# Attention output split from its accumulation bank into projection operands; gate tiles by block; chain sums by transfer

## The chip, the cores and the metric

The kernel runs on one core of a Trainium2 chip. The metric is device time in microseconds (us) of one execution. The engines are TensorE (PE, with its weight loads PEld), VectorE (DVE), ScalarE (ACT), GpSimd (POOL, which here mostly issues transfers) and SyncE (SP, which issues the loads and stores). Every engine works through its own queue of instructions in order; the queues meet at semaphores.

## The reference

One step of a layer of a streaming encoder in float32, over T = 16 + 1024 + 32 = 1072 tokens (16 meta tokens, 1024 frames of a new stream, 32 frames of a running one), model width 1024:

```python
h = rmsnorm(x, g)
a_in, q, k, v = split(h @ w_in, [1024, 1536, 1664])          # ONE input projection, 1792 columns
glu  = a_in[..., :512] * sigmoid(a_in[..., 512:])
a    = silu(layernorm(depthwise_causal_conv(glu, width=31)))  # group A, 512 channels
# group B: 8 query heads, 2 key/value heads of 64; chunks of 64 tokens see the 16 meta
# tokens, the two chunks before and their own; a bias by distance; one sink per head
s = q @ k.T * 64**-0.5 + bias
m = maximum(max(s), sink);  p = exp(s - m)
o = (p / (sum(p) + exp(sink - m))) @ v
x = x + concat([a, o]) @ w_out                                # 1024 x 1024
u = rmsnorm(x) @ w_up                                         # 2 x 2816 columns
x = x + (silu(depthwise_causal_conv(u[:2816], width=3)) * u[2816:]) @ w_down
y = rmsnorm(x)
```

The new keys, values and convolution states are outputs too.

## The kernel before

**Layout.** All activations are feature-major: 128 partitions of features, so that 1024 features are eight k-tiles, and tokens along the free axis. Tokens go in three blocks, 336, 384 and 352 wide in the input projection (`TB`) and 324, 384 and 352 (the chunks' own borders: `OB`) or with their halos in the stages behind it.

**Precision.** Each float32 operand of a large product is two parts: `hi`, a cast to a narrower form of float32 that PE takes in one pass, and `lo`, the rest. A k-step of such a product is three matmuls, hi by hi, lo by hi and hi by lo (`mm3`, L255 to L257). `hi` is always a cast on ACT. `lo` is made in one of two ways: by a subtraction on DVE (`split`, L249 and L250; for weights L242), or by a negation on ACT (L244) and a transfer from POOL's queue that adds the raw operand to it.

**Input projection.** Its 14 column tiles of 128 are the keys, the values, four of queries, and for each of the four channel tiles of group A a value and a gate tile. Twelve are done ahead of the attention loop. The last two, gate and value of channel tile 3, are a generator, `glu_stream`, which the attention loop draws on for k-steps to fill PE. It does all three blocks of the one tile, then all three of the other. When a block's sums are ready, ACT and DVE turn them into gated values (`flush`), and the convolution taps of this channel and block can start.

**Convolution.** 31 taps on DVE for each channel tile and token range, each one multiply-add over a row of up to 1090 values (L400 for the first, L403 for the others). They are put into DVE's queue at a lower priority than all else, so the scheduler places them where it expects DVE to be free. A table `TA` says how many microseconds' worth of taps each iteration of the loop may bring. For one channel tile, the taps 1 to 20 of its second and third block are made in another way, the "chain": ACT multiplies, and transfers add the products up in the halves of a buffer. At the end of iteration `CHE` = 5 two DVE additions (L434) add these sums to the accumulator.

**The attention loop.** Eighteen jobs (the meta tokens, eleven chunks, the running stream, five chunks), and two more iterations to drain, as a pipeline of three stages. Iteration i does, in this written order:

1. for job i-1: the reciprocals of the softmax sums on DVE (L769), and the normalisation of four probability tiles, the last `SCA[i]` of them on ACT (L774), the others on DVE (L772);
2. for job i: the scores on PE (L802), bias and row minimum on DVE (L757), the exponentials on ACT (L764);
3. for job i-2: the value products on PE (L837, L841), into one half of the accumulation bank called `o`; the two halves take turns from job to job;
4. for job i-1: the transposes of the probabilities on PE (L821, L823) and their copy to the operand of the value product on ACT (L828);
5. for job i-2: `keep`, which copies the value products from the bank into the float32 buffer `CA` on ACT (L845);
6. `FILL[i]` k-steps of `glu_stream`, the evacuation of sums that are ready, and `taps(TA[i])`.

In this region PE and ACT go in the written order, and DVE in the order that the scheduler chose. When `glu_stream` has ended, the iterations go on with the generator `later` (it closes the pool "h" that holds the input projection's operands `hi` and `lo`, opens the pools of the next stage in its place, and prepares weights) and with the first groups of the output projection's attention half, block 0.

**From the loop to the output projection.** `ca_split` (L935, L936, L940) turns `CA` block by block into the operands `CAH` and `CAL`: for block 0's first half and block 1's second half by ACT (cast and negation) and an adding transfer, otherwise by ACT's cast and DVE's subtraction (L250). `later` calls it for blocks 0 and 1 inside the loop, and for block 2 it is called behind the loop. The attention half of the output projection follows (PE, mainly), with the convolution's layer norm beside it, then its convolution half, then the feed-forward part.

The lines that matter most here:

```python
def keep(self, t=None, n=64):
    nc.scalar.copy(CA[:, :, self.tok:self.tok + n],
                   self.o[:, :4 * n].rearrange("p (a b) -> p a b", a=4))
def chain_end():
    for a, half in chain:
        nc.vector.tensor_tensor(out=a, in0=a, in1=half, op=ALU.add)
```

Of the kernel before, what the change touches and what calls it, by code (L numbers as in the profile page):

```python
# [54 lines left out]
TA = [2.01, 2.74, 5.63, 6.64, 4.22, 3.28, 2.42, 2.68, 2.08, 1.57, 2.08, 2.08, 3.18, 1.41, 2.1, 0.85, 4.71, 3.21, 5.98, 2.57]  # L55
# [17 lines left out]
SCA = [1, 2, 2, 2, 1, 1, 2, 2, 2, 2, 2, 1, 2, 2, 0, 1, 1, 2, 2, 2]  # L73
# [6 lines left out]
CHE = 5  # L80
# [4 lines left out]
CSD = ['12', '00']  # L85
AH = (1, 2, 1, 3, 5, 4, 5)
AG = (('00', '02'), ('h',), ('l',), ('10',), ('12',))
# [82 lines left out]
def body(nc, tc, cp, wp, xp, dp, io):  # L170
# [36 lines left out]
    cH, ph = pool("h", "right")  # L207
    HI, LO = [None] * 3, [None] * 3
    for z, name, b in ((HI, "hi", 0), (HI, "hi", 2), (LO, "lo", 2), (HI, "hi", 1), (LO, "lo", 1), (LO, "lo", 0)):
        z[b] = new(ph, f"{name}{b}", KD, TB[b][1], dt=F32R)  # L210
# [221 lines left out]
    def chain_end():  # L432
        for a, half in chain:
            nc.vector.tensor_tensor(out=a, in0=a, in1=half, op=ALU.add)  # L434
        chain.clear()
# [352 lines left out]
    class Chunk:  # L788
# [55 lines left out]
        def keep(self, t=None, n=64):  # L844
            nc.scalar.copy(CA[:, :, self.tok:self.tok + n],  # L845
                           self.o[:, :4 * n].rearrange("p (a b) -> p a b", a=4))
# [65 lines left out]
    def glu_stream():  # L912
        w = nxt
        for i, c in enumerate(order[NPRE:]):
            for b in range(3):
                for k, ps in enumerate(in_mm(b, w, lead(c, b))):
                    if k == 2 and b == 0:
                        wn = take()
                    if k == 2 and b == 1:
                        fetch()  # L920
# [3 lines left out]
            w = wn  # L924
        woas.append(w)
# [3 lines left out]
    CAH, CAL, woas = [], [], []  # L929

    def ca_split(b, k0, k1, dma=False):
        t0, n = OB[b]
        for k in range(k0, k1):
            if dma:
                nc.scalar.copy(CAH[b][:, k, :], CA[:, k, t0:t0 + n])  # L935
                nc.scalar.activation(CAL[b][:, k, :], CA[:, k, t0:t0 + n], AF.Copy, scale=-1.0)  # L936
            else:
                split(CAH[b][:, k, :], CAL[b][:, k, :], CA[:, k, t0:t0 + n])
        if dma:
            nc.gpsimd.dma_start(CAL[b][:, k0:k1, :], CA[:, k0:k1, t0:t0 + n], accum_op=ALU.add)  # L940

    def after_glu():
# [8 lines left out]
        for step in AG:  # L951
            for op in step:
# [9 lines left out]
                else:  # L962
                    while op[0] == "1" and kept[0] < 11:
                        yield
# [933 lines left out]
```

## Time and profile before

| | |
|---|---|
| runs | 1049.37, 1050.64, 1051.31 us (median 1050.64) |
| profiled execution | 1049.64 us, its span 1047.9 us |
| PE, PEld busy | 1030.4 us (98%), 1004.3 us |
| DVE, ACT, POOL busy | 864.3 us (82%), 507.0 us (48%), 163.8 us (16%) |
| transfers | 124.41 MB, 119 GB/s in the mean |
| attention loop | from 163.5 us (first scores) to 248.3 us (last value products) |

The span is the time from the first to the last instruction that the profile holds; what lies around it (1.74 us here) belongs to the execution too. Line numbers are those of the kernel before. In a row of a window or a timeline the first figure is the start in us and the second the duration. In a row of a group of instructions, the figures behind the bar are the busy time in us, the mean duration of one in ns, and the idle time of the engine just ahead of them, with what ended most of it.

### The profile page before, as it was taken

How to read it: one execution, taken by the hardware profiler on the slowest of the kernel's cores; microseconds unless marked ns; L12 is line 12 of the kernel's file. 1: busy time of each engine (PE TensorE's matmuls, PEld its weight loads, DVE VectorE, ACT ScalarE, POOL GpSimd, SP SyncE). 2: the span in 40 equal slices, each digit the busy share in tenths (PEclk: the TensorE clock that was granted, in tenths of full speed). 3: DMA queues.
4: the chain of work that ended last, by engine and by line, in shares of the span. 5: the costliest groups of instructions: out<-in, count | busy, mean ns of one | idle time of the engine just before them, and what ended most of it. 6: DMA issues, size and time to landing. Idle time of an engine off the chain costs nothing.

```text
span 1047.9 us, 19995 instructions
## 1 busy us (share of the span) xinstructions
PE 1030.4 (98%) x7747; PEld 1004.3 (96%) x7747; DVE 864.3 (82%) x1649; ACT 507.0 (48%) x1074; POOL 163.8 (16%) x205
## 2 busy tenths in 40 slices
PE   9999999989999999999999999999999999999997
PEld 8999998758999999999999999999999999999997
DVE  7999988899978978878888888888777976986636
ACT  8653336896675644433333343343336722532334
POOL 1133220002335210001000110100010041000043
PEclk9999999999999999999999999999999999999999
DMA  7388673124953213242233234232326795732204
GB/s 268 90 172 163 147 152 79 41 55 72 171 152 109 68 63 102 76 140 93 72 124 113 64 101 116 89 103 85 120 72 210 247 190 127 247 125 68 95 2 166
DMA packets 69047, 124.41 MB, mean 119 GB/s; under 512 B 10448, under 2 KB 42568, under 8 KB 68952
## 3 DMA queue, kind: packets, MB, share of 16 engines
q1 hardware_dynamic: 56392, 97.77, 28.9%
q0 software_dynamic: 12128, 24.95, 14.0%
q8 instruction: 61, 1.00, 0.4%
q10 hardware_dynamic: 432, 0.41, 0.1%
q14 instruction: 34, 0.28, 0.1%
HBM read 79.42 MB, written 27.51 MB: 102 GB/s over the span
## 4 chain that ended last, share of the span: by engine, by line
PE 86%; ACT 6%; DVE 6%; DMA 2%; issue 1%; SPq 0%; DVEq 0%; ACTq 0%
PE mm L1282 51%; PE mm L255 10%; PE mm L256 10%; PE mm L257 10%; ACT pb L764 1%; DVE acc L403 1%; ACT glu L828 1%; DVE bl L1219 1%; DVE x L1424 1%; PE R L292 1%; ACT hi L341 1%; PE R L271 1%; DMA xs<-xT 0%; DMA gx<-yq 0%; ACT glu L764 0%
## 5 line engine op out<-in xcount | busy, mean ns | idle before, releaser
L1282 PE MATMUL mm<-bh,sl 128*128 128x264 f32 (+1 forms) x912 | 214.0, 284 | 0.0
L1282 PEld LDWEIGHTS mm<-bh,sl 128*128 128x128 f32 x912 | 157.2, 188 | 0.0
L403 DVE SCALAR_TENSOR_TENSOR acc<-glu,prm,acc 128x324 f32<-128x324 f32 (+4 forms) x190 | 155.3, 846 | 1.1
L1282 PE MATMUL mm<-bl,sl 128*128 128x264 f32 (+1 forms) x424 | 120.9, 285 | 0.0
L1282 PE MATMUL mm<-th,rawr 128*128 128x264 f32 x640 | 120.0, 284 | 0.0
L1282 PE MATMUL mm<-bh,wlo 128*128 128x264 f32 (+1 forms) x440 | 117.6, 284 | 0.0
L1424 DVE TENSOR_TENSOR x<-x,mm 128x264 f32<-128x264 f32 (+7 forms) x238 | 76.8, 351 | 44.4 <-PE mm L1282 44.3
L1282 PE MATMUL mm<-bh,whi 128*128 128x264 f32 (+1 forms) x440 | 112.6, 284 | 0.7 <-DVE x L1424 0.7
L255 PE MATMUL mm<-hi,whi 128*128 128x352 f32 (+3 forms) x312 | 103.9, 333 | 0.4 <-ACT hi L341 0.4
L256 PE MATMUL mm<-lo,whi 128*128 128x352 f32 (+3 forms) x312 | 101.2, 324 | 0.2 <-DVE lo L342 0.2
L257 PE MATMUL mm<-hi,wlo 128*128 128x352 f32 (+3 forms) x312 | 101.2, 324 | 0.0
L1282 PEld LDWEIGHTS mm<-th,rawr 128*128 128x128 f32 x640 | 100.4, 188 | 0.0
L1282 PE MATMUL mm<-th,sl 128*128 128x264 f32 x352 | 92.7, 284 | 0.0
L1282 PE MATMUL mm<-tl,rawr 128*128 128x264 f32 x320 | 90.8, 284 | 0.0
L1282 PEld LDWEIGHTS mm<-bh,wlo 128*128 128x128 f32 x440 | 80.6, 188 | 0.0
L1282 PEld LDWEIGHTS mm<-bl,sl 128*128 128x128 f32 x424 | 79.9, 188 | 0.0
L1282 PEld LDWEIGHTS mm<-bh,whi 128*128 128x128 f32 x440 | 79.0, 188 | 0.9 <-issue 0.9
L1282 PE MATMUL mm<-bl,whi 128*128 128x264 f32 (+1 forms) x272 | 77.5, 285 | 0.0
L1218 ACT CAST sl<-x 128x512 fp32r<-128x512 f32 (+1 forms) x41 | 29.7, 727 | 73.2 <-DMA x<-wup 37.6
L1282 PEld LDWEIGHTS mm<-th,sl 128*128 128x128 f32 x352 | 63.8, 188 | 0.0
L1282 PEld LDWEIGHTS mm<-tl,rawr 128*128 128x128 f32 x320 | 60.3, 188 | 0.0
L255 PEld LDWEIGHTS mm<-hi,whi 128*128 128x128 f32 x312 | 58.7, 188 | 1.6 <-issue 0.6
(400 smaller groups left out, 2925.7 us busy)
## 6 DMA issues: line engine op xcount, KB each, us to landing
x<-wup SPq DMA_DIRECT2D x20, 512.0 KB, 4.1
x<-wup SPq DMA_DIRECT2D x40, 256.0 KB, 2.8
yq<-x SPq DMA_DIRECT2D x32, 264.0 KB, 2.8
wlo<-raw POOLq DMA_DIRECT2D x16, 512.0 KB, 4.6
ca<-ca POOLq DMA_DIRECT2D x18, 383.0 KB, 5.1
raw<-win SPq DMA_DIRECT2D x12, 512.0 KB, 4.4
raw<-wdn SPq DMA_DIRECT2D x12, 512.0 KB, 3.5
rb<-yq SPq DMA_DIRECT2D x10, 528.0 KB, 4.4
```

Of the source, the lines that this page charges most:

```text
L255: nc.tensor.matmul(ps, whi(k), xhi(k), start=first and i == 0, stop=False)
L256: nc.tensor.matmul(ps, whi(k), xlo(k), start=False, stop=False)
L257: nc.tensor.matmul(ps, wlo(k), xhi(k), start=False, stop=last and i == n - 1)
L271: nc.tensor.matmul(ss[:, i:i + 1], z[:, at:at + P], ones[:, 0:1], start=j == 0, stop=j == len(parts) - 1)
L292: nc.tensor.matmul(R[:, at:at + P], left[i], diag[i], start=True, stop=True)
L341: hid[b, k] = nc.scalar.activation(HI[b][:, k, :], X[b][:, k, :], AF.Copy, scale=pcol("g1", k)).ins
L403: nc.vector.scalar_tensor_tensor(out=a, in0=e[:, a0 + k:a1 + k], scalar=pcol("cw", p * CW + k), in1=a, op0=ALU.mult, op1=ALU.add)
L764: nc.scalar.activation(qs_[i], qs_[i], AF.Exp, bias=m[0][:, i:i + 1], scale=-1.0, accum_out=m[1][:, i:i + 1])
L828: nc.scalar.copy(ptb[kv], pts[kv])
L1218: nc.scalar.copy(hi, raw)
L1282: nc.tensor.matmul(ps, w[:, j, :], x[:, j, :], start=first and j + i == 0, stop=j == 3 and i == 2, skip_group_check=True)
L1424: summed[0] = nc.vector.tensor_tensor(out=z, in0=z, in1=ps[:, lo_:hi_], op=ALU.add).ins
```

## The change

The value products no longer go through `CA`. The tile set of `lo` moves to the pool of the next stage's accumulator `X` (pool "x1", whose tiles have the same size and take `lo`'s place later), and `hi` stays in the pool "h". `CAH[b]` and `CAL[b]` become views of `hi` of block b: k-tiles 0 to 3 and 4 to 7. `keep` casts from the bank on ACT straight into `CAH`, and subtracts on DVE, from the bank, into `CAL`. `ca_split`, the pool "cas" and the list `CSD` are gone, and so are the casts, negations, subtractions and adding transfers that they issued.

As `hi` of a block can be overwritten only when both remaining column tiles have read it, `glu_stream` now goes block by block: both tiles of block 0, both of block 1, both of block 2. For this the second tile's weight is loaded and split ahead of the loop, its low part by DVE. The output projection's first groups in the loop wait for job 5 to be kept, in place of the splits.

The chain's two sums are added by transfers from POOL's queue at the end of iteration 3. The table of the taps' budget and that of the normalisations on ACT (`SCA`) are new: by index, iterations 11, 14, 15 and 16 have one more on ACT.

```diff
@@ -52,7 +52,7 @@
 NPB = 8
 TGS = [3.0, 3.0, 1000.0, 1000.0]
 TGW = [3.0, 5.0, 6.5, 3.5, 1000.0, 1000.0, 5.0, 1000.0, 1000.0, 1000.0, 3.5, 3.5, 1000.0, 1000.0, 1000.0, 1000.0, 1000.0, 1000.0, 3.0, 3.0, 1000.0, 1000.0, 1000.0, 1000.0, 1000.0, 1000.0, 7.0, 3.5, 3.5, 3.5]
-TA = [2.01, 2.74, 5.63, 6.64, 4.22, 3.28, 2.42, 2.68, 2.08, 1.57, 2.08, 2.08, 3.18, 1.41, 2.1, 0.85, 4.71, 3.21, 5.98, 2.57]
+TA = [2.01, 1.4, 2.2, 0.6, 1.4, 1.0, 2.4, 2.0, 1.7, 1.5, 1.6, 1.7, 1.9, 1.7, 1.7, 1.5, 2.6, 2.4, 3.5, 2.5]
 TH = 5.9
 WAYS = 2
 BS = ((0, 2), (1, 0), (2, 1), (2, 2))
@@ -70,21 +70,20 @@
 WLD = True
 MANUAL = {mybir.EngineType.PE, mybir.EngineType.Activation}
 MANEND = MANUAL | {mybir.EngineType.DVE}
-SCA = [1, 2, 2, 2, 1, 1, 2, 2, 2, 2, 2, 1, 2, 2, 0, 1, 1, 2, 2, 2]
+SCA = [1, 2, 2, 2, 1, 1, 2, 2, 2, 2, 2, 2, 2, 2, 1, 2, 2, 2, 2, 2]
 LN0 = 14
 LNS = 21
 FILL = [4, 6, 6, 2, 3, 3, 6, 1, 3, 3, 1, 4, 5, 0, 3, 6, 0, 3, 0, 3]
 ORDER = [2, 3, 8, 9, 4, 5, 10, 11, 12, 13, 6, 7]
 CHAINS = ((0, 1),)
 CHN = 1
-CHE = 5
+CHE = 3
 CHK = 21
 CHT = 0
 CHG = (1, 2)
 SEGS = (((0,), (1, 2)), ((0, 1, 2),), ((0, 1, 2),), ((0,), (1,), (2,)))
-CSD = ['12', '00']
 AH = (1, 2, 1, 3, 5, 4, 5)
-AG = (('00', '02'), ('h',), ('l',), ('10',), ('12',))
+AG = (('h',), ('l',))
 AT = (1, 8)
 AT2 = 13
 AFE = (0, 3, 18, 19)
@@ -204,10 +203,10 @@
 
     rbt = new(xp, "rb", T)
     rb = [rbt[:, t0:t0 + n] for t0, n in TB]
-    cH, ph = pool("h", "right")
-    HI, LO = [None] * 3, [None] * 3
-    for z, name, b in ((HI, "hi", 0), (HI, "hi", 2), (LO, "lo", 2), (HI, "hi", 1), (LO, "lo", 1), (LO, "lo", 0)):
-        z[b] = new(ph, f"{name}{b}", KD, TB[b][1], dt=F32R)
+    cX, px = pool("x1", "right")
+    LO = [new(px, f"x{b}", KD, n, dt=F32R) for b, (t0, n) in enumerate(TB)]
+    cS, ph = pool("h", "right")
+    HI = [new(ph, f"hi{b}", KD, n, dt=F32R) for b, (t0, n) in enumerate(TB)]
     cC, pc = pool("acc", "left")
     acc = new(pc, "acc", NCV, ACCW)
     cG, pg = pool("glu", "left")
@@ -431,7 +430,7 @@
 
     def chain_end():
         for a, half in chain:
-            nc.vector.tensor_tensor(out=a, in0=a, in1=half, op=ALU.add)
+            nc.gpsimd.dma_start(a, half, accum_op=ALU.add)
         chain.clear()
 
     def taps(us, behind=None):
@@ -842,8 +841,11 @@
                                      stop=True)
 
         def keep(self, t=None, n=64):
-            nc.scalar.copy(CA[:, :, self.tok:self.tok + n],
-                           self.o[:, :4 * n].rearrange("p (a b) -> p a b", a=4))
+            b = 0 if self.tok < OB[1][0] else 1 if self.tok < OB[2][0] else 2
+            lo_ = max(self.tok, OB[b][0])
+            o = self.o[:, :4 * n].rearrange("p (a b) -> p a b", a=4)[:, :, lo_ - self.tok:]
+            at = slice(lo_ - OB[b][0], self.tok + n - OB[b][0])
+            split(CAH[b][:, :, at], CAL[b][:, :, at], o)
 
     class Meta(Chunk):
         def __init__(self):
@@ -910,44 +912,31 @@
             Chunk.keep(self, n=NS)
 
     def glu_stream():
-        w = nxt
-        for i, c in enumerate(order[NPRE:]):
-            for b in range(3):
-                for k, ps in enumerate(in_mm(b, w, lead(c, b))):
-                    if k == 2 and b == 0:
-                        wn = take()
-                    if k == 2 and b == 1:
-                        fetch()
+        cs = order[NPRE:]
+        ws = {cs[0]: nxt}
+        for b in range(3):
+            for c in cs:
+                for k, ps in enumerate(in_mm(b, ws[c], lead(c, b))):
+                    if k == 0 and b == 0 and c == cs[0]:
+                        ws[cs[1]] = take(dve=True)
+                    if k == 2 and c == cs[1]:
+                        if b < 2:
+                            fetch()
+                        else:
+                            wn = take()
                     if k == KD - 1:
                         pend.append((c, b, ps))
                     yield
-            w = wn
-        woas.append(w)
+        woas.append(wn)
 
     stream = glu_stream()
     jobs = [Meta()] + [Chunk(c) for c in range(11)] + [Sample()] + [Chunk(c) for c in range(11, NCH)]
-    CAH, CAL, woas = [], [], []
-
-    def ca_split(b, k0, k1, dma=False):
-        t0, n = OB[b]
-        for k in range(k0, k1):
-            if dma:
-                nc.scalar.copy(CAH[b][:, k, :], CA[:, k, t0:t0 + n])
-                nc.scalar.activation(CAL[b][:, k, :], CA[:, k, t0:t0 + n], AF.Copy, scale=-1.0)
-            else:
-                split(CAH[b][:, k, :], CAL[b][:, k, :], CA[:, k, t0:t0 + n])
-        if dma:
-            nc.gpsimd.dma_start(CAL[b][:, k0:k1, :], CA[:, k0:k1, t0:t0 + n], accum_op=ALU.add)
+    CAH, CAL = ([z[:, i:i + 4, :OB[b][1]] for b, z in enumerate(HI)] for i in (0, 4))
+    woas = []
 
     def after_glu():
-        nonlocal X, cX, cS
-        close(cH)
-        cX, px = pool("x1", "right")
+        nonlocal X
         X = [new(px, f"x{b}", KD, n) for b, (t0, n) in enumerate(OB)]
-        cS, pcs = pool("cas", "right")
-        for b, (t0, n) in enumerate(OB):
-            CAH.append(new(pcs, f"cah{b}", 4, n, dt=F32R))
-            CAL.append(new(pcs, f"cal{b}", 4, n, dt=F32R))
         for step in AG:
             for op in step:
                 if op == "h":
@@ -959,11 +948,6 @@
                     nc.gpsimd.dma_start(lo, raw, accum_op=ALU.add)
                     woas.append((hi, lo))
                     fetch()
-                else:
-                    while op[0] == "1" and kept[0] < 11:
-                        yield
-                    ca_split(int(op[0]), int(op[1]), int(op[1]) + 2, op in CSD)
-                    halved[0] += op[0] == "0"
             yield
 
     def halves(w):
@@ -986,7 +970,7 @@
 
     def ah_stream():
         for m2 in range(2):
-            while halved[0] < 2 or not woas:
+            while kept[0] < 5 or not woas:
                 yield
             woav[m2] = halves(woas.pop(0))
             for i in range(2):
@@ -995,9 +979,8 @@
                         adds.append((m2, i, 0, ps))
                     yield
 
-    woav, adds, kept, halved = {}, [], [-1], [0]
+    woav, adds, kept = {}, [], [-1]
     ahs = ah_stream()
-    cX = cS = None
     later = after_glu()
 
     a, z = None, None
@@ -1037,8 +1020,7 @@
                 ah_add(*q)
             adds.clear()
         if i == CHE:
-            with tc.issue_after(job.q[1][3]):
-                chain_end()
+            chain_end()
         z, a = a, job
     for _ in later:
         pass
@@ -1086,7 +1068,6 @@
                 for lo_, hi_, o in pieces(b, 0, SOFF, OB):
                     split(CVH[b][:, p, lo_:hi_], CVL[b][:, p, lo_:hi_], acc[:, p, o:o + hi_ - lo_])
 
-    ca_split(2, 0, 4)
     close(cD)
     close(cA)
     lns = [ln(b) for b in range(3)]
```

In the changed kernel the line numbers are lower by one up to about line 930.

**VectorE at the start of the loop**, before; `qs` is the last query tile, L403 a tap (1090 columns: three blocks at once), L757 the first job's bias and minimum (`S` are scores, `sm` the softmax's small numbers), L575 and L632 the evacuation of a gate tile:

```order
L605 SCALAR_TENSOR_TENSOR qs<-mm,rb 128x32
L403 SCALAR_TENSOR_TENSOR acc<-glu,prm,acc 128x1090 x2
L757 ISA glu,sm<-S,bme 128x17
L757 ISA sm 128x1
L575 TENSOR_TENSOR glu<-mm,rb 128x336
L403 SCALAR_TENSOR_TENSOR acc<-glu,prm,acc 128x1090
L769 RECIPROCAL sm<-sm 128x1
L632 SCALAR_TENSOR_TENSOR glu<-glu,rb 128x336
```

and in the changed kernel:

```order
L604 SCALAR_TENSOR_TENSOR qs<-mm,rb 128x32
L402 SCALAR_TENSOR_TENSOR acc<-glu,prm,acc 128x1090
L241 TENSOR_TENSOR wlo<-raw,whi 128x1024
L402 SCALAR_TENSOR_TENSOR acc<-glu,prm,acc 128x1090
L756 ISA glu,sm<-S,bme 128x17
L756 ISA sm 128x1
L574 TENSOR_TENSOR glu<-mm,rb 128x336
L402 SCALAR_TENSOR_TENSOR acc<-glu,prm,acc 128x1090
L768 RECIPROCAL sm<-sm 128x1
```

The low part of the second weight (`wlo`) now stands between the last two long taps ahead of the first softmax, and the gating of the first block comes later.

**VectorE behind the last reciprocal**, in the tail of the loop, before (L772 are two normalisations, `pb` and `glu` their tiles; taps of the second and third block, 384 and 382 columns):

```order
L769 RECIPROCAL sm<-sm 128x4
L403 SCALAR_TENSOR_TENSOR acc<-glu,prm,acc 128x384
L403 SCALAR_TENSOR_TENSOR acc<-glu,prm,acc 128x382
L772 TENSOR_SCALAR pb_307<-pb_307,sm 128x209
L772 TENSOR_SCALAR glu<-glu,sm 128x209
L403 SCALAR_TENSOR_TENSOR acc<-glu,prm,acc 128x384
L403 SCALAR_TENSOR_TENSOR acc<-glu,prm,acc 128x382
L403 SCALAR_TENSOR_TENSOR acc<-glu,prm,acc 128x384
```

and in the changed kernel (`hi_90` is block 2's tile, its upper half the operand `CAL`, its lower half `CAH`; L249 is `keep`'s subtraction, from the bank `o`):

```order
L768 RECIPROCAL sm<-sm 128x4
L402 SCALAR_TENSOR_TENSOR acc<-glu,prm,acc 128x384
L402 SCALAR_TENSOR_TENSOR acc<-glu,prm,acc 128x382
L771 TENSOR_SCALAR pb_310<-pb_310,sm 128x209
L771 TENSOR_SCALAR glu<-glu,sm 128x209
L402 SCALAR_TENSOR_TENSOR acc<-glu,prm,acc 128x384
L249 TENSOR_TENSOR hi_90<-o,hi_90 128x4x64
L402 SCALAR_TENSOR_TENSOR acc<-glu,prm,acc 128x382
L402 SCALAR_TENSOR_TENSOR acc<-glu,prm,acc 128x384
L402 SCALAR_TENSOR_TENSOR acc<-glu,prm,acc 128x382
```

A subtraction stands three instructions behind the normalisations' start, seven taps follow (the last rows shown and four more), then the next subtraction, four taps, and in between the layer norm's additions the last one.

**TensorE in an iteration of the loop**, before: the last k-step of the stream's filler (`mm`, block 2), the scores `S` of a job, the value products into `o`, the first transpose into `pt`:

```order
L257 MATMUL mm<-hi_83,wlo 128x352
L802 MATMUL S<-kT,qp 128x209 [waits DVE_49] x2
L802 MATMUL S<-kT,qp 128x209 x2
L837 MATMUL o<-glu,va 64x256 [waits Activation_49]
L837 MATMUL o<-glu,va 64x256
L841 MATMUL o<-glu,vb 64x256 x2
L821 MATMUL pt_1720<-ident,pb_305 128x128 [waits DVE_49]
```

and in the changed kernel:

```order
L256 MATMUL mm<-hi_90,wlo 128x352
L801 MATMUL S<-kT,qp 128x209 [waits DVE_49] x2
L801 MATMUL S<-kT,qp 128x209 x2
L836 MATMUL o<-glu,va 64x256 [waits DVE_49]
L836 MATMUL o<-glu,va 64x256 [waits Activation_49]
L840 MATMUL o<-glu,vb 64x256 x2
L820 MATMUL pt_1723<-ident,pb_308 128x128
```

The first value product of a job now waits on DVE (the subtraction of the job before, from the same bank), the second on ACT; before, the first waited on ACT and the transposes on DVE. Apart from the order of the stream's k-steps, PE's instructions are the same, 6799 rows in each.

## The prediction, made before the changed kernel had run

> **What bounds the kernel now.** I read the page first, for the engine that is never idle and for the slices where it is.
>
> ```profile
> span 1047.9 us, 19995 instructions
> PE 1030.4 (98%) x7747; PEld 1004.3 (96%) x7747; DVE 864.3 (82%) x1649; ACT 507.0 (48%) x1074; POOL 163.8 (16%) x205
> PE   9999999989999999999999999999999999999997
> DVE  7999988899978978878888888888777976986636
> ACT  8653336896675644433333343343336722532334
> ```
>
> TensorE is the bound everywhere but in a few slices: one slice in the first half and the last one fall below 9. In the first half these are the attention loop's, and there VectorE and ScalarE stand at 7 to 9 too. The loop is also all that the change touches, so next I cut it by windows: the last taps ahead of it, the loop up to its ninth reciprocal, on to its eighteenth and last, its tail, and the two stages behind it.
>
> ```profile
> core 0: us, PE busy (x) PEld busy (x) DVE busy (x) ACT busy (x) POOL busy (x), PEclk, DMA share, GB/s
> 160.90:163.50 2.60, 2.60 (x18) 2.44 (x16) 2.56 (x4) 1.37 (x2) 0.85 (x1) 1.00 0.30 114
> 163.50:201.90 38.40, 36.52 (x267) 29.13 (x267) 31.72 (x121) 30.82 (x106) 0.85 (x1) 1.00 0.23 56
> 201.90:242.60 40.70, 35.81 (x269) 25.86 (x268) 40.47 (x150) 38.35 (x124) 3.31 (x3) 1.00 0.24 46
> 242.60:248.30 5.70, 5.55 (x42) 4.04 (x40) 5.70 (x14) 3.90 (x10) 1.46 (x2) 1.00 0.43 57
> 248.30:297.40 49.10, 49.10 (x308) 48.40 (x309) 41.87 (x92) 32.26 (x66) 18.11 (x17) 1.00 0.77 133
> ```
>
> Behind the loop PE is busy 49.10 of 49.10 us: what ends the loop earlier or later moves everything behind it by as much. In the loop the two halves differ. In the first (38.40 us) PE is nearest to full, 36.52, and DVE has 6.7 us to spare. In the second (40.70 us) DVE is full, 40.47, ACT has 38.35, PE only 35.81: DVE sets the pace there. The clock is 1.00 in all rows. These marks of DVE bound the halves and the tail:
>
> ```profile
> 201.90 0.18 DVE L769 RECIPROCAL sm<-sm 128x4 f32<-128x4 f32 x1
> 242.56 0.16 DVE L769 RECIPROCAL sm<-sm 128x4 f32<-128x4 f32 x1
> 242.64 1.10 DVE L403 SCALAR_TENSOR_TENSOR acc<-glu,prm,acc 128x384 f32<-128x384 f32 x2
> 244.15 4.83 DVE L403 SCALAR_TENSOR_TENSOR acc<-glu,prm,acc 128x384 f32<-128x384 f32 x9
> ```
>
> **The change part by part.** Prices of single instructions:
>
> ```profile
> L403 DVE SCALAR_TENSOR_TENSOR acc<-glu,prm,acc 128x324 f32<-128x324 f32 x60 | 33.1, 551 | 0.4
> L403 DVE SCALAR_TENSOR_TENSOR acc<-glu,prm,acc 128x384 f32<-128x384 f32 x30 | 18.3, 610 | 0.0
> L772 DVE TENSOR_SCALAR pb<-pb,sm 128x209 f32<-128x209 f32 x25 | 7.2, 323 | 0.1
> L1424 DVE TENSOR_TENSOR x<-x,mm 128x264 f32<-128x264 f32 x96 | 40.9, 428 | 30.9 <-PE mm L1282 30.7
> L1424 DVE TENSOR_TENSOR x<-x,mm 128x208 f32<-128x208 f32 x32 | 11.7, 367 | 0.0
> L242 DVE TENSOR_TENSOR wlo<-raw,whi 128x1024 fp32r<-128x1024 f32 x2 | 2.4, 1222 | 0.7 <-ACT whi L240 0.7
> L250 DVE TENSOR_TENSOR cal<-ca,cah 128x324 fp32r<-128x324 f32 x2 | 0.9, 495 | 0.0
> L434 DVE TENSOR_TENSOR acc<-acc,ca 128x766 f32<-128x766 f32 x2 | 1.9, 956 | 0.0
> ```
>
> Nine taps back to back take 4.83, 0.54 each, where one alone has 0.61: behind another, an instruction costs 0.07 less than its row. So a tap is 0.48 (324 columns) or 0.54 (384), a normalisation 0.25, a weight's low part 1.15, a chain sum 0.89, an old attention subtraction 0.43 to 0.49. The new subtraction, 4x64 columns read from the bank, has no row. It lies between the additions of 208 and 264 columns that also read a bank, 0.367 and 0.428, nearly at the upper: 0.42, or 0.35 behind another.
>
> First half, by the instruction order from the two long taps ahead of the first softmax to the ninth reciprocal: taps of 324 columns go from 11 to 21 and of 384 from 0 to 6, since the last channel tile's first block is gated sooner (+4.8 and +3.2); six subtractions are new, one of them small (+1.85); the second gate weight's low part comes from ACT and a transfer to DVE (+1.15); two chain sums leave (-1.8); three gate pieces come later (-0.5). Sum +8.7. DVE had 2.56 + 31.72 = 34.3 busy in the 41.0 us from 160.9; it now needs 43.0. Its spare 6.7 us are used up and 2.0 are missing. PE's work in this half is the same to a few tenths, ACT loses two of four sigmoid pieces. I take **+2.0**. Lower end +1.4, if the new subtractions cost no more than 0.25; upper +3.2, if DVE still waits 1.2 us for scores behind the iteration with 18 projection matmuls.
>
> Second half, ninth to last reciprocal: taps of 324 from 20 to 10, of 384 from 21 to 15, of 382 from 3 to 6 (-4.8, -3.2, +1.6); four normalisations go to ACT (-1.0); four old subtractions leave (-1.8); nine new ones come (+3.0, one of half width); three gate pieces come (+0.5). Sum -5.7: DVE falls from 40.5 to 34.8. What is then late next is ACT:
>
> ```profile
> L240 ACT CAST whi<-raw 128x1024 fp32r<-128x1024 f32 x17 | 17.9, 1051 | 25.4 <-PE mm L256 24.8 <-PE pt L256 0.6
> L244 ACT ACTIVATE wlo<-raw 128x1024 fp32r<-128x1024 f32 x15 | 15.9, 1061 | 0.0
> L774 ACT ACTIVATE pb<-pb,sm 128x209 f32<-128x209 f32 x16 | 7.2, 489 | 0.0
> L935 ACT CAST cah<-ca 128x384 fp32r<-128x384 f32 x2 | 1.1, 547 | 0.0
> L936 ACT ACTIVATE cal<-ca 128x384 fp32r<-128x384 f32 x2 | 1.1, 563 | 0.0
> ```
>
> On ACT an instruction behind another costs about 0.1 less than its row (the windows view gives 38.35 for what the rows would put higher). Eight casts and four negations leave, half of them 324 wide (-4.9); a second weight pair falls into this half (+1.9); four normalisations come (+1.5); gate pieces (+0.5). Net -1.0, to 37.4. The cast into the operand replaces the old copy one for one. So the floor is 37.4 and the ceiling what it is now, 40.7. PE has 35.8. ACT's idle time now is 2.35 us, all of it beside a full DVE; with DVE 3 us freer I leave 0.7 of it: 38.1, **-2.6**.
>
> The tail is where the new wait bites. PE already waits for the attention bank's reader:
>
> ```profile
> PEld o L837 <- ACT ca L845: 6.9, 11, 1.1
> PE o L837 <- ACT ca L845: 3.5, 9, 0.8
> 243.38 0.65 PE L837 MATMUL o<-glu,va 128*64 128x256 f32 x4 [0.15 <-ACT ca L845]
> 247.21 0.65 PE L837 MATMUL o<-glu,va 128*64 128x256 f32 x4
> 247.69 0.60 PE L841 MATMUL o<-glu,vb 81*64 81x256 f32 x4
> ```
>
> These value products write one half of the bank, and wait for the ACT copy that read the other half for the chunk before. The Trainium skill, "PSUM — Partial Sum Buffer", section "PSUM bank collisions raise a hardware error", says the same as a rule: guard by bank and quadrant, not by address, since two engines in one bank collide even at other columns. It speaks against this change, which adds a second reader to that bank; the trace agrees, with 11 waits of up to 1.1 us for the first reader.
>
> After the change PE waits for the subtraction, and DVE reaches that only in its queue's order. In the tail this is, from the last reciprocal: two taps (1.1), two normalisations (0.5), a tap (0.54), the subtraction (0.35), then seven taps (3.8) and the next subtraction. So the next-to-last value product starts 2.5 us behind the reciprocal instead of 0.8 (243.38 against 242.56). The last one starts after the second subtraction at 6.6 instead of 4.65 (247.21 against 242.56). **+1.8**, with ends 0 (if these subtractions came ahead of the taps) and +2.2. Queued behind it on PE are the 24 first matmuls of the next block.
>
> Edits at no cost. The two chain sums become accumulating transfers; such transfers took 5.1 us from issue to landing, and their result is first read by the layer norm:
>
> ```profile
> ca<-ca POOLq DMA_DIRECT2D x18, 383.0 KB, 5.1
> 248.90 0.48 DVE L1056 TENSOR_TENSOR glu<-acc 128x324 f32<-128x324 f32 x1
> ```
>
> They are issued in the fourth iteration, some 60 us ahead; without that cover they would cost 2 x 5.1. On POOL's queue they stand before the low parts of two weights, which come over 20 us later; SP's queue is unchanged. Behind the loop DVE is about 2 us lighter, which gains nothing while PE is full; the last subtraction, 9.9 us behind the reciprocal, is needed 24 matmuls behind the last value product, at 11.6, so 1.7 us cover it.
>
> Sum: +2.0 - 2.6 + 1.8 = **+1.2 us**. Span 1047.9 to 1049.1. The profiled execution's own time is 1049.64, 1.74 above its span, and the median of the runs is 1.0 above that: 1050.64 + 1.2 = **1051.8 us**.
>
> **The rivals.** *The second half gains nothing* (chance 0.30). Mechanism: the subtraction stands in DVE's queue behind the normalisations, and needs ACT's cast behind the probability copies; the value products, transposes and then the next scores wait for it in each of nine iterations. It decides from the point where 0.35 us per iteration is added: 9 x 0.35 = 3.2 eats the 2.6. For it: the 11 waits above, on the faster reader. Against it: PE has 4.9 us spare in that half. Time: +2.0 + 0 + 1.8 = +3.8, 1054.4.
>
> *The floors are reached* (0.22). DVE's extra early taps fill only gaps, the first half stays at its 38.4, the second falls to ACT's 37.4, and the tail's waits vanish: 0 - 3.3 + 0 = 1047.3. For it: ACT sheds its bursts of casts in the middle of the loop. Against it: 43.0 us of DVE work in 41.0, all ahead of the ninth reciprocal in one queue.
>
> *The edit does not do what it says* (0.03): the removed splits are simply replaced, work for work, and the loop keeps its length, 1050.6.
>
> **How the numbers follow.** Forecast 0.45, its own range 1049.8 to 1053.8 from the three terms' nearer ends. Taken with the rivals I state 1047.4 to 1055.0: it takes in both rivals, and leaves a tenth outside on each side. Changes under 0.2% (2.1 us) cannot be told from none here. Slower by more: most of the first rival and a fifth of the forecast, 0.33. Faster by more: the second rival, 0.22. Within: 0.45.
>
> **What would show it.** First half: the ninth reciprocal near 203.9 and DVE busy all through. Second half: 38 us, ACT the fullest. Tail: the last value product 6.6 us behind the last reciprocal, and waits of PE on the subtraction in the place of those on the ACT copy. Wrong would be a ninth reciprocal before 202, a second half under 37 or over 40, or any change of length behind the loop.

## The result, and the profile after

The changed kernel is slower: median 1060.73 us (1054.86 to 1062.64, six runs) against 1050.41 us (1049.37 to 1052.09, six runs), 10.3 us more. The ratio of the runs' means is 1.0086, with a 95% interval of 1.006 to 1.0112; it lies under that of the medians (1.0098), since two of the six runs were clearly faster than the rest. The forecast was 1051.8, its range went up to 1055.0.

The windows view of the changed kernel, cut at the same marks as before: the last long taps and the loop to its ninth reciprocal, on to the eighteenth, the tail to the end of the last value product, and the stage behind.

```profile
core 0: us, PE busy (x) PEld busy (x) DVE busy (x) ACT busy (x) POOL busy (x), PEclk, DMA share, GB/s
160.90:206.90 46.00, 42.09 (x284) 33.61 (x283) 42.20 (x142) 29.48 (x103) 1.71 (x2) 0.93 0.16 36
206.90:252.37 45.47, 38.42 (x262) 28.34 (x261) 36.29 (x142) 37.72 (x120) 1.71 (x2) 0.89 0.21 48
252.37:260.07 7.70, 6.68 (x49) 5.09 (x47) 7.70 (x19) 4.04 (x11) 1.68 (x2) 1.00 0.32 44
260.07:309.20 49.13, 49.13 (x310) 48.43 (x311) 38.46 (x83) 30.62 (x62) 17.93 (x17) 1.00 0.74 131
```

Before, these pieces took 41.0 us (38.40 and the 2.60 ahead of it), 40.7, 5.7 and 49.1. So the first half lost 5.0 us, the second 4.8, the tail 2.0, and the stage behind nothing. The loop as a whole lost 11.8 us, and the span of the profiled execution grew by 11.1 (1047.9 to 1059.0). Two things are new. No engine is full in either half: VectorE, which was full in the second half, is busy 36.29 us of 45.47 there and 42.20 of 46.00 in the first, ScalarE 37.72 in the second. And the granted clock, 1.00 in all rows before, is 0.93 and 0.89.

The waits in the loop name what TensorE stood for (total, times, longest); before, the two rows of this kind had 6.9 and 3.5 us on ScalarE's copy:

```profile
PEld o L836 <- DVE hi L249: 12.5, 11, 3.5
PE o L836 <- DVE hi L249: 9.1, 7, 3.2
```

This is the wait that was forecast for the tail, the value products behind the subtraction from the same bank; but most of it lies inside the loop. The costliest place but one is the fifth iteration. TensorE's timeline there (start, duration, in brackets the idle time ahead and what ended it):

```profile
178.92 0.98 PE L801 MATMUL S<-kT,qp 64*128 64x209 f32 x8
181.83 1.12 PE L836 MATMUL o<-glu,va 128*64 128x256 f32 x4 [1.94 <-DVE hi L249]
182.88 1.12 PE L840 MATMUL o<-glu,vb 17*64 17x256 f32 x4
```

and ScalarE's cast and what VectorE did in the meantime:

```profile
179.65 0.38 ACT L248 CAST hi<-o 128x256 fp32r<-128x256 f32 x1
...
179.59 0.56 DVE L402 SCALAR_TENSOR_TENSOR acc<-glu,prm,acc 128x324 f32<-128x324 f32 x1
180.06 0.32 DVE L771 TENSOR_SCALAR glu<-glu,sm 128x209 f32<-128x209 f32 x1
180.30 0.56 DVE L771 TENSOR_SCALAR pb<-pb,sm 128x209 f32<-128x209 f32 x2
180.77 0.37 DVE L756 CUSTOM_DVE_ANT_0 pb<-S,bt 128x209 f32<-128x209 f32 x1
...
181.36 0.42 DVE L249 TENSOR_TENSOR hi<-o,hi 128x256 fp32r<-128x256 f32 x1
```

The cast was done at 180.03 (179.65 and 0.38), and the bank would have been free there if ScalarE had been its only reader. VectorE comes to the subtraction only behind three normalisations and two bias operations, at 181.36. TensorE stands idle for 1.94 us, about 1.8 of them behind the cast's end. In the longest wait (3.16 us, up to 220.34) the cast ended at 218.32, so that some 2.0 us belong to the subtraction; the time before would have passed with one reader too. Then the fifth iteration's value products take 1.12 us where they took 0.65 before. The clock explains that. The windows around the three longest waits, cut where the granted clock changes:

```profile
178.28:181.70 3.42, 1.62 (x13) 1.04 (x11) 3.42 (x15) 3.05 (x11) 0.00 (x0) 1.00 0.00 0
181.70:185.11 3.41, 3.28 (x14) 1.76 (x15) 3.41 (x14) 1.51 (x7) 0.00 (x0) 0.50 0.00 0
185.11:188.52 3.41, 3.41 (x13) 3.16 (x11) 1.99 (x5) 1.82 (x4) 0.00 (x0) 0.50 0.00 0
188.52:191.94 3.42, 3.42 (x28) 2.51 (x28) 2.68 (x11) 1.86 (x9) 0.00 (x0) 1.00 0.00 0
215.83:219.24 3.41, 1.35 (x11) 0.80 (x9) 2.28 (x13) 3.41 (x12) 0.00 (x0) 1.00 0.81 154
219.24:222.66 3.42, 2.32 (x10) 1.19 (x11) 2.69 (x8) 1.63 (x8) 0.00 (x0) 0.50 0.46 158
222.66:226.07 3.41, 3.41 (x16) 3.41 (x15) 0.43 (x1) 1.45 (x3) 0.00 (x0) 0.50 0.00 0
232.90:236.31 3.41, 1.80 (x19) 1.11 (x17) 2.79 (x15) 3.15 (x12) 0.00 (x0) 1.00 0.81 154
236.31:239.72 3.41, 3.41 (x18) 3.13 (x14) 2.19 (x7) 2.38 (x9) 0.00 (x0) 0.50 0.58 154
```

In all three places a stretch of 3.41 us in which TensorE was busy for 1.35 to 1.80 us is followed by one or two such stretches at half clock. TensorE was busy for 15.8 us at half clock (3.28, 3.41, 2.32, 3.41, 3.41), work that takes half as long at full clock: 7.9 us lost, by this count, beside the idle time itself.

### The profile page after: what moved, and what is told of

Same layout as the page of the kernel before. It is cut to its first block, busy times and chain, and to the rows that moved or that the text cites. A ratio compares the mean times of both kernels' runs of the same rounds, so it can differ in the third digit from the quotient of the medians.

```text
span 1059.0 us, 19999 instructions
## 1 busy us (share of the span) xinstructions
PE 1037.4 (98%) x7747; PEld 1010.2 (95%) x7747; DVE 865.4 (82%) x1654; ACT 502.2 (47%) x1061; POOL 162.5 (15%) x204
## 4 chain that ended last, share of the span: by engine, by line
PE 87%; DVE 4%; ACT 3%; issue 2%; DMA 2%; POOL 0%; POOLq 0%; DVEq 0%; ACTq 0%
PE mm L1263 54%; PE mm L254 9%; PE mm L255 9%; PE mm L256 9%; DVE acc L402 2%; DMA ca<-ca 1%; DVE pb L756 1%; PE R L291 1%; ACT hi L340 1%; PE R L270 1%; PE S L801 1%; DMA raw<-woc 1%; DMA xs<-xT 0%; PE pt L820 0%; ACT pb L763 0%
## 5 line engine op out<-in xcount | busy, mean ns | idle before, releaser
L254 PE MATMUL mm<-hi,whi 128*128 128x384 f32 (+3 forms) x408 | 138.3, 339 | 0.2 <-ACT hi L340 0.2
L256 PE MATMUL mm<-hi,wlo 128*128 128x384 f32 (+3 forms) x408 | 133.2, 326 | 0.0
L255 PE MATMUL mm<-x,whi 128*128 128x384 f32 (+3 forms) x312 | 102.2, 327 | 0.2 <-DVE x L341 0.2
L254 PEld LDWEIGHTS mm<-hi,whi 128*128 128x128 f32 x408 | 77.9, 191 | 2.2 <-issue 1.0
L256 PEld LDWEIGHTS mm<-hi,wlo 128*128 128x128 f32 x408 | 77.6, 190 | 0.0
```

Of the source, the lines that this page charges most:

```text
L254: nc.tensor.matmul(ps, whi(k), xhi(k), start=first and i == 0, stop=False)
L255: nc.tensor.matmul(ps, whi(k), xlo(k), start=False, stop=False)
L256: nc.tensor.matmul(ps, wlo(k), xhi(k), start=False, stop=last and i == n - 1)
```

## The experiments

Theory: the subtraction is a second reader of the value products' bank, and TensorE waits for it in VectorE's queue order; the waits cost their own length, and where they leave TensorE idle for about half of a 3.41 us stretch, they cost half clock as well. Rivals: the heavier load of VectorE in the first half and the moved work of ScalarE; the new tables; the clock as a mere sign of idle time, without a price of its own.

**The subtraction away from the bank.** In `keep`, of the changed kernel:

```diff
-            split(CAH[b][:, :, at], CAL[b][:, :, at], o)
+            ca = CA[:, :, lo_:self.tok + n]
+            nc.scalar.copy(ca, o)
+            split(CAH[b][:, :, at], CAL[b][:, :, at], ca)
```

> The changed kernel, but the value products are first copied from the bank into the old float32 buffer by ScalarE, and cast and subtraction read that buffer. TensorE then waits for a copy of ScalarE again, not for the subtraction; ScalarE has 17 more casts of about 0.36 us (some 6 us in the loop), all else is as in the changed kernel. Theory (TensorE's wait for the subtraction starts the loss, and where it is idle for 1.6 us or more inside some 3.4 us its granted clock falls to half for one or two such stretches): no wait of value products on the subtraction, clock 1.00 in the loop, loop some 8 to 11 us shorter, 1050 to 1053 us. Rival (the loss is the heavier VectorE load of the first half and the moved work of ScalarE): 1058 to 1062 us, rather more than less, since ScalarE has more to do.

Measured: 1050.51 us, ratio to the kernel before 1.0004 (95% interval 0.9995 to 1.0014; so in all that follows). The loop's waits of value products now name ScalarE's copy, and the second half's window shows the clock at 1.00 and a new bound:

```profile
PE o L836 <- ACT ca L849: 3.4, 6, 1.2
...
202.65:243.20 40.55, 35.05 (x263) 24.86 (x263) 36.44 (x142) 40.26 (x129) 1.71 (x2) 1.00 0.24 54
```

So some 10 us hang on the wait and what follows from it, although ScalarE has more to do. But nothing is won against before: ScalarE, with 17 more instructions, is as full (40.26 of 40.55) as VectorE was.

**Filling the waits.** The changed kernel with useless transposes ahead of the value products in three iterations:

```diff
+        if i in (4, 11, 14):
+            for _ in range(16):
+                nc.tensor.transpose(pts[0][:, 0, 0:128], ident, ident)
         if z:
             z.outs()
```

> The changed kernel with 16 useless transposes (about 1.8 us at full clock) put on TensorE's queue ahead of the value products of iterations 4, 11 and 14, where the profile showed TensorE idle for 1.94, 3.16 and 1.61 us and then at half clock for 6.85, 6.8 and 3.4 us. Nothing else is changed. Theory: the waits stay, but are filled; the clock stays at 1.00 there, and of the 7.9 us that the half clock cost most come back: 1053 to 1056 us, though TensorE does 5 us of useless work more. Rival (the clock only follows the waits and costs nothing of its own): 1060 to 1064 us.

Measured: 1054.13 us, 1.0041 (1.0026 to 1.0056), with 48 useless instructions more. That is 6.6 us faster than the changed kernel by the medians, 5.3 by the means, 6.0 in the profiled executions. The same place on TensorE's timeline, then the two halves and the tail at this run's own marks:

```profile
179.01 0.98 PE L801 MATMUL S<-kT,qp 64*128 64x209 f32 x8
179.92 1.97 PE L1001 MATMUL pt<-ident 128*128 128x128 f32 x16
181.92 0.65 PE L836 MATMUL o<-glu,va 128*64 128x256 f32 x4
...
160.90:203.92 43.02, 41.01 (x301) 33.23 (x300) 41.78 (x143) 29.58 (x103) 1.70 (x2) 1.00 0.17 40
203.92:245.38 41.46, 37.99 (x294) 28.28 (x293) 36.27 (x141) 37.51 (x120) 1.71 (x2) 1.00 0.22 53
245.38:253.09 7.71, 6.69 (x49) 5.10 (x47) 7.71 (x19) 4.05 (x11) 1.68 (x2) 1.00 0.31 46
```

The value products start as late as they did (181.92 against 181.83), but at full clock. The first half is 3.0 us shorter than in the changed kernel, the second 4.0, the tail the same. The half clock has a price of its own. The count above (7.9) puts it too high; why was not followed.

**The tables.** The changed kernel with `TA` and `SCA` of before:

```diff
-TA = [2.01, 1.4, 2.2, 0.6, 1.4, 1.0, 2.4, ...]
-SCA = [1, 2, 2, 2, 1, 1, 2, 2, 2, 2, 2, 2, 2, 2, 1, 2, 2, 2, 2, 2]
+TA = [2.01, 2.74, 5.63, 6.64, 4.22, 3.28, 2.42, ...]
+SCA = [1, 2, 2, 2, 1, 1, 2, 2, 2, 2, 2, 1, 2, 2, 0, 1, 1, 2, 2, 2]
```

> The changed kernel with the tables of before for the taps' budget and for the normalisations on ScalarE; the subtraction from the bank stays. Theory: waits for the subtraction stay, and grow, since more taps stand ahead of it in the first half; 1060 to 1068 us, with half-clock stretches in the loop. Rival (the new tables are what costs): 1050 to 1055 us.

Measured: 1063.96 us, 1.0134 (1.0119 to 1.015). The wait of value products on the subtraction grows, the longest to 3.6 us:

```profile
PEld o L836 <- DVE hi L249: 17.3, 12, 3.6
```

The new tables are not the cause; they took 3 us off the loss.

**Everything but the new path.** The kernel before with the block-wise `glu_stream`, both new tables, the second weight's low part on VectorE and the chain sums by transfer:

```diff
-CHE = 5
+CHE = 3
-            nc.vector.tensor_tensor(out=a, in0=a, in1=half, op=ALU.add)
+            nc.gpsimd.dma_start(a, half, accum_op=ALU.add)
...
```

> The kernel before with everything of the change except the attention output's path: gate tiles by block, the second weight's low part on VectorE, both new tables, and the chain sums by transfer; value products still go through the float32 buffer and are split from it. Theory: no half clock, 1049 to 1053 us. Rival (the reordered gating overloads VectorE in the first half): 1055 us or more.

Measured: 1052.32 us, 1.0024 (1.0013 to 1.0035), with the clock at 1.00 throughout the loop and the ninth reciprocal at 201.85. All these parts together cost 2.4 us, not ten. The execution that was profiled is the slowest of this run (1054.05), with a span 4.3 us above that of before: 1.0 of them in the second half, where ScalarE is now full (41.53 of 41.71), as the old splits and the new table both burden it, 0.5 in the tail and 2.9 behind the loop. The last were not followed.

**A second reader and nothing else.** The kernel before, with a useless subtraction per chunk that reads the bank, and its twin that reads ScalarE's copy in `CA`, outside the banks:

```diff
             nc.scalar.copy(CA[:, :, self.tok:self.tok + n], ...)
+            nc.vector.tensor_tensor(out=scr[:, :, :min(n, 56)],
+                in0=self.o[...][:, :, :min(n, 56)],              # the twin: in0=CA[...]
+                in1=CA[:, :, self.tok:self.tok + min(n, 56)], op=ALU.subtract)
```

> The kernel before, unchanged in its work, plus a useless VectorE subtraction per chunk that reads the bank of the value products (4x56 columns, against the copy that ScalarE made of it) and writes to a scratch tile. So the bank has a second reader, on VectorE, and the next value products wait for it. VectorE gets 18 instructions of some 0.35 us more, about 6 us, of which 3 in its full second half. Theory: waits of value products on VectorE, some above 1.6 us, and half-clock stretches after these: 1055 to 1062 us. Rival (only VectorE's load counts): 1052 to 1054 us, as its twin that reads the copy.

> The twin: the same useless subtractions at the same places of VectorE's queue, reading the copy in SBUF instead of the bank. TensorE doesn't wait for them. Theory: VectorE's second half is longer by up to 3 us, the clock stays at 1.00: 1051 to 1054 us, and well below the run that reads the bank. Rival (load alone): the same as that run within 1.5 us.

Measured: 1059.61 us, 1.0096 (1.0075 to 1.0116), for the bank; 1051.93 us, 1.002 (1.001 to 1.003), for the copy. The same instructions at nearly the same places of the queue differ by 7.7 us. First the waits of the run that reads the bank and its clock around three of them, then the same of the twin:

```profile
PE o L838 <- DVE scr L848: 11.9, 8, 3.3
...
222.85:226.26 3.41, 0.46 (x4) 0.34 (x6) 3.41 (x15) 3.41 (x12) 0.00 (x0) 1.00 0.25 39
226.26:229.67 3.41, 3.41 (x16) 2.17 (x13) 2.41 (x9) 1.54 (x5) 0.00 (x0) 0.50 0.00 0
236.50:239.91 3.41, 1.75 (x16) 1.23 (x16) 3.28 (x14) 3.41 (x12) 0.00 (x0) 1.00 0.53 148
239.91:243.33 3.42, 3.42 (x27) 2.69 (x29) 3.42 (x11) 3.42 (x13) 1.20 (x1) 1.00 0.20 37
243.33:246.74 3.41, 1.19 (x12) 0.80 (x14) 3.41 (x15) 2.79 (x10) 0.00 (x0) 1.00 0.53 88
246.74:250.15 3.41, 3.41 (x18) 2.47 (x15) 3.41 (x11) 1.63 (x7) 0.00 (x0) 0.50 0.00 0
```

```profile
PE o L838 <- ACT ca L846: 3.5, 8, 1.1
...
211.61:215.02 3.41, 1.78 (x16) 0.85 (x14) 3.41 (x14) 3.41 (x14) 0.00 (x0) 1.00 0.00 0
215.02:218.44 3.42, 2.83 (x21) 2.53 (x21) 3.38 (x12) 2.46 (x8) 0.00 (x0) 1.00 0.03 5
```

The twin has one stretch of 3.41 us with TensorE as little busy (1.78), but keeps its clock in this execution (1051.57 us, mean granted clock 0.999). Not in every one: its four slowest, 1052.66 to 1054.75 us, have means of 0.997 and 0.996, against 0.996 to 0.993 in all four runs that read the bank. In the run that reads the bank only two stretches ran at half clock, 3.4 us by the count above; the rest of its loss is the waits themselves. So the second reader of the bank alone, without any other part of the change, makes a loss of nearly the same size.

**A bank for each parity.** The changed kernel with its work unchanged; odd and even jobs write banks of their own:

```diff
-        return pa.tile([P, 512], F32, tag="mm", name="mm", bufs=3)
+        turn[0] = (turn[0] + 1) % 3
+        if wide[0] and turn[0] == 2:          # not during the loop
+            return pa.tile([P, 512], F32, tag="o2", name="mm")
+        return pa.tile([P, 512], F32, tag="mm", name="mm", bufs=2)
-        return obank[:, onum[0] % 2, :]
+        return obanks[onum[0] % 2][:, 0, :]   # tags "o" and "o2"
```

> The changed kernel with its work unchanged, but each half of the value products' bank is a bank of its own: odd jobs write one, even jobs the other, and the second one is taken from the three banks of the projection's sums for the length of the loop. The value products then wait for the subtraction of two jobs ago, which is done long before. Theory: no wait of value products on the subtraction, no half clock; with the wait gone the forecast's other terms hold, ninth reciprocal 1 to 2 us later than before, second half near 38 us since ScalarE bounds it, tail as before: 1047.5 to 1050 us. Rival (two banks are too few for the projection's sums in the loop): new waits of matmuls on evacuations, 1052 us or more.

Measured: 1048.08 us, 0.998 (0.9971 to 0.9989): faster than both kernels. The windows at its own marks:

```profile
160.90:202.70 41.80, 40.74 (x293) 32.99 (x292) 41.40 (x142) 29.95 (x104) 1.71 (x2) 1.00 0.18 44
202.70:240.61 37.91, 35.28 (x263) 25.33 (x263) 35.28 (x141) 36.75 (x119) 1.71 (x2) 1.00 0.24 58
240.61:246.16 5.55, 5.55 (x42) 4.09 (x41) 5.55 (x15) 3.94 (x11) 1.48 (x2) 1.00 0.41 56
```

The first half is 0.8 us longer than before, the second 2.8 shorter with ScalarE the fullest, the tail 0.2 shorter, and the clock 1.00. The two banks left for the projection's sums are enough: the waits of this loop name no matmul of theirs that waits for an evacuation, and no value product that waits for the subtraction.

The control is the kernel before with the same two banks:

> The kernel before with two banks for the value products, and nothing else: the control for the two-bank version of the change. Its value products no longer wait for ScalarE's copy of the job before (11 waits of up to 1.1 us in the trace of before). If those waits, and not the change's own moves of work, were what the two-bank version won: 1047.5 to 1049 us here too. Theory (the second half of the kernel before is bound by a full VectorE, 40.5 us busy, whatever TensorE waits for): 1049.5 to 1050.5 us, no difference from before.

Measured: 1050.6 us, 1.0002 (0.9993 to 1.0011). The gain is not that of the second bank alone.

**Cast and subtraction elsewhere.** ScalarE copies the bank to `CA` as in the first experiment; the cast, and in one version the subtraction too, go to GpSimd:

```diff
-            split(CAH[b][:, :, at], CAL[b][:, :, at], o)
+            ca = CA[:, :, lo_:self.tok + n]
+            nc.scalar.copy(ca, o)
+            nc.gpsimd.tensor_copy(CAH[b][:, :, at], ca)
+            nc.vector.tensor_tensor(out=CAL[b][:, :, at], in0=ca, ...)   # or nc.gpsimd
```

> As the decoupled version (ScalarE's copy from the bank, subtraction on VectorE from the copy), but the cast on GpSimd instead of ScalarE: ScalarE is lighter by some 6 us than there. If ScalarE's second reading was what ate the gain of the decoupled version: 1047 to 1049 us. If not: 1050 to 1051 us.

> The changed kernel with the value products copied from the bank by ScalarE into the old float32 buffer, and both parts (cast and subtraction) made from it on GpSimd, which has little to do in the loop. TensorE waits for ScalarE's copy alone, and VectorE loses its 17 subtractions (about 5.5 us), ScalarE the extra casts of the decoupled version. If VectorE and ScalarE were the bound of the loop once the waits are gone, it beats both kernels: 1046 to 1049 us. If the loop is bound by the round of scores, softmax and transposes, it is 1049 to 1051 us. If GpSimd's work slows VectorE by sharing its port, 1051 to 1056 us.

> The version with ScalarE's copy and GpSimd's cast, with two loads moved: the table of before for the normalisations, so four go back from ScalarE to VectorE in the second half, where ScalarE had 37.1 us busy of 37.8 and VectorE 35.8; and the subtractions of the first seven jobs on GpSimd, where VectorE had 41.9 of 42.1. If the busiest engine bounds each half, the first is 41 to 41.5 us from the mark, the second 37 us: 1046 to 1048 us. If the round of scores, softmax and transposes bounds them, 1048 to 1049 us as without.

Measured: 1048.09 us, 0.9984 (0.9974 to 0.9993), with the cast alone on GpSimd; 1049.81 us, 0.9996 (0.9987 to 1.0006), with both there; 1049.74 us, 0.9998 (0.999 to 1.0007), with the normalisations' old table and only the first eight subtractions (the meta tokens' and seven chunks') on GpSimd. The second half of each:

```profile
203.04:240.81 37.77, 34.05 (x260) 24.61 (x260) 35.75 (x142) 37.12 (x119) 5.55 (x11) 1.00 0.25 58
...
202.07:240.35 38.28, 34.19 (x261) 24.58 (x261) 35.92 (x132) 37.18 (x120) 11.62 (x20) 1.00 0.25 57
...
202.27:241.42 39.15, 35.23 (x267) 25.45 (x267) 36.79 (x143) 36.33 (x116) 6.91 (x13) 1.00 0.24 56
```

The first beats the kernel before, as expected. The second won nothing, the middle one of its three expected cases. The third was a miss: 1049.74 lies above both of its ranges. Taking the subtractions off VectorE does not lighten it as counted (35.92 beside 35.75 us, though 3.6 us of subtractions have left it). VectorE's other instructions got longer: the same 31 taps took 17.90 us there and 16.56 with the cast alone on GpSimd. Four taps of 384 columns took 2.59 us where a whole subtraction of GpSimd ran beside them (from 214.36), and 2.14 where one was nearly over (from 218.57). So GpSimd's subtraction slows VectorE, as one of the expectations had it; through what, no run here shows. Giving four normalisations back makes the second half longer (39.15) though both engines have over 2 us to spare, so that the sum of the work does not set its length there; what does was not followed. The loop of the version with both parts on GpSimd ended 1.8 us earlier than before's (at 246.5), but the stages behind took 1.1 us more; why is open.

## Why the prediction was wrong

**The prices and the sums held.** The new subtraction took 0.42 us (forecast 0.42). With the wait gone, in the run with a bank for each parity, VectorE's second half has 35.3 us (forecast 34.8) and ScalarE's 36.8 (37.4), and that half lasts 37.9 (38.1): the term of -2.6 measures -2.8. The first half's term was too high: +0.8 against +2.0, since VectorE, full there as forecast, needed 41.4 us and not 43.0. The chain sums by transfer and the lighter VectorE behind the loop cost and gained nothing that shows.

**The tail held.** Its two value products, and the subtractions ahead of them, stand where the prediction put them, at 2.6 and 6.6 us behind the last reciprocal (252.37):

```profile
254.49 0.41 DVE L249 TENSOR_TENSOR hi<-o,hi 128x256 fp32r<-128x256 f32 x1
254.96 0.65 PE L836 MATMUL o<-glu,va 128*64 128x256 f32 x4 [0.88 <-DVE hi L249]
254.82 3.77 DVE L402 SCALAR_TENSOR_TENSOR acc<-glu,prm,acc 128x382 f32<-128x382 f32 x7
258.52 0.41 DVE L249 TENSOR_TENSOR hi<-o,hi 128x256 fp32r<-128x256 f32 x1
258.98 0.65 PE L836 MATMUL o<-glu,va 128*64 128x256 f32 x4
```

Forecast +1.8 (6.6 against 4.65 makes 1.95), measured +2.0.

**The step that failed** is "The tail is where the new wait bites". The wait was read off VectorE's queue for the tail and charged nowhere else: the two halves were sums of busy time, in which a wait has no place. In the loop the trace shows the same as in the tail. The subtraction stood behind normalisations and bias operations in the fifth iteration, and behind bias operations and two taps ahead of 219.87; each time TensorE waited 1.8 to 2.0 us longer than for the cast. Against the kernel before, the halves came out at +5.0 and +4.8 us, where +2.0 and -2.6 were forecast.

The first rival named just this mechanism, with a chance of 0.30, and gave it 0.35 us in each of nine iterations, the length of the subtraction. The trace shows fewer and longer waits, since their price is the queue ahead of the subtraction. In sum the rival was near: with the waits filled and the clock kept, the second half took 41.46 us, 3.5 more than the 37.91 without waits, against its 3.2, and the time was 1054.1, against its 1054.4. That this first half was +2.0 as well is luck: VectorE's load made 0.8 of them, the waits 1.2.

**What the prediction did not have at all** is the clock. "The clock is 1.00 in all rows" was read as a fact of the kernel, not as something that its lack of idle time bought. Before, the longest wait of the value products was 1.1 us. The change brought three places where TensorE was idle for about half of a 3.41 us stretch or more, and the half clock behind these is the other 5 to 7 us. None of the stated ends would have covered it: even the upper ends of the three terms together (+3.2, 0 and +2.2) lead to 1056.0.

With the waits filled the kernel stayed just inside the range; with the half clock it left it. What the bare waits cost is not fixed as closely as that. Of the six runs of the changed kernel, four had a mean granted clock of 0.990 to 0.993 and took 1060.7 to 1062.6 us. One had 0.997 and took 1054.9, and one had 0.998 and took 1057.6, outside the range. Nearly all runs of the kernel before have 0.997 to 0.999. No trace of the last two was kept, so the 1057.6 stays open.

**The bank as the unit of a wait.** The sentence from the Trainium skill ("PSUM — Partial Sum Buffer", section "PSUM bank collisions raise a hardware error"), to guard by bank, was read the right way round, and the pair of useless subtractions shows it cleanly (1059.6 against 1051.9 us). In this program, whose semaphores make TensorE wait, a reader in the same bank holds up a writer of the other half, and the same work outside the bank does not.

**The marks named in advance.** The second half was over 40 us, which the prediction had named as a sign of being wrong. Its signs of being right failed in the first half, with the ninth reciprocal at 206.9 where 203.9 was forecast and VectorE not busy all through, and in the second, where ScalarE was busy only 37.72 us of 45.47. A ninth reciprocal that came late was not among the signs of being wrong, only an early one. The last value product 6.6 us behind the last reciprocal, waits on the subtraction in the place of those on the copy, and no change behind the loop, were right.

## What to carry to other kernels

When a buffer gets a second reader, price the wait by what stands in that reader's queue ahead of it, in every iteration, and not by the length of the reading instruction; a bank per parity took the whole wait away here. Treat a granted clock of 1.00 as something that can be lost: list the idle stretches of TensorE before the change, and ask which of them the change makes longer. Give each half of a loop its waits as well as its work. A sum of busy times is a floor that a loop reaches only when its waits are short: here it was right within 1.2 us for each half once the wait was gone, and 3.0 and 7.4 us off with it.

## What the runs showed of the hardware that was not expected

The granted clock changed in steps that lie 3.41 us apart or a multiple of it, and fell to exactly half. The Trainium skill, "TensorE: Matmul & The Clock Gate", section "What's actually happening", describes such windows, of about 3.4 us and running freely, and has the clock fall after at least one idle window. The length agrees; the condition was easier to meet here. A window in which TensorE was busy for 1.62, 1.35, 1.80, 0.46 or 1.19 us was enough, so about half idle and not all. It is no sharp border: windows with 1.75 us busy (the run that reads the bank) and 1.78 us busy (the twin) kept the clock, while one with 1.80 lost it, so the busy time of the trace alone does not decide it.

How long it stays at half differs, one window or two. In the second case of the changed kernel the first slow window still held a wait; in the first case it did not, but eight of its matmuls were value products, some on 17 rows only, so that the reason is open. A wait that falls across a window's border is divided between two windows, which may be why the changed kernel's six runs lie 7.8 us apart, with mean clocks from 0.990 to 0.998, and those of before 2.7; no run here separates this.
